# The low parts of the SSD weights: from a GpSimd subtraction to a ScalarE negation and an adding DMA

## The chip, the cores and the metric

The kernel runs on one core of a Trainium2 chip. The metric is the device time of one execution in microseconds, the median of several runs. The core has five instruction streams that run beside each other and meet through semaphores: TensorE (PE, with PEld for its weight loads), VectorE (DVE), ScalarE (ACT), GpSimd (POOL) and SyncE (SP), which only issues DMAs. DMAs can also be issued from ScalarE and GpSimd; all are carried out by the same 16 DMA engines.

## The reference: two layers of a hybrid decoder

One inference step runs 512 prompt tokens and 8 x 8 sample tokens (576 rows of width 1024) through two layers. Each layer has a token mixer between two half-step SwiGLU FFNs; layer 0 mixes with an SSD (Mamba-2) mixer, layer 1 with a pooling mixer. All is in float32. The change touches the SSD mixer:

```python
proj = h @ w_in                                   # 1024 -> 2048 (z) + 4096 (x, B, C) + 32 (dt)
xbc, conv_new = causal_dwconv(xbc, conv0, conv_w, conv_b); xbc = silu(xbc)
dt = softplus(dt_raw + dt_bias);  A = -exp(a_log)
y, ssm_new = ssd_scan(xs, dt, A, Bm, Cm, ssm0)    # 32 heads in 8 groups, chunks of 128
y = (y + d_skip * xs) * silu(z);  y = grouped_rmsnorm(y) * norm_g
return y @ w_out                                  # 2048 -> 1024
```

## The kernel before

Activations lie in SBUF with features on the 128 partitions and 576 tokens along the free dimension, in two halves of 288. A float32 product is made of three passes in a faster, rounded format (fp32r): every operand is split into a high part (the rounded value) and a low part (what the rounding left), and the matmuls are high x high, high x low and low x high. `mm` (line 334) does this: for each 128-row slice of a weight it issues six matmuls of 128x288, two halves times three products.

**Weights.** `load` (line 321) brings a slab of raw weights from HBM into one of two `raw` buffers, with a DMA from SyncE's queue. `unit` (line 328) cuts it into blocks of at most four 128x128 slices. `block` (line 311) splits one into a `wb` tile with both parts; the pool `spl` has six of them. Line 317 is ScalarE's cast to the high part, line 318 the subtraction that makes the low part, on VectorE or, where the caller says so, on GpSimd. A `wb` buffer comes free when TensorE has used it; a `raw` buffer when the low part has been made.

**The SSD stage** (`ssd`). `proj` computes 128 output features of `w_in` from the eight slices of a unit, so two blocks and 48 matmuls; 48 such units are used, 46 of them through `unit(..., G)` inside `proj` (two are prepared before, on VectorE). `outproj` adds products with `w_out` to the residual `x`: 32 units of one block, 8 of them with two slices and 24 with four. Between these, `conv_in` (lines 629 to 647) turns a projection into a convolved row block, a chain of VectorE instructions with line 645 the longest; lines 702 to 766 make the decay factors of all heads once, a chain of small 128x160 VectorE instructions (706 to 721), a spill to DRAM from ScalarE's queue (725, 727), exponentials (733, 735) and small TensorE products (746 on); and `pair` does the scan of two heads, 16 times, with masks on GpSimd (803 to 805), ten exponentials on ScalarE (808) and loads of `m`, `eb` and `nat` from SyncE's queue (795, 798, 779). `rstd` (lines 187 to 198) makes a reciprocal root by a chain of 128x5 VectorE instructions, once for each of the groups' norms.

**Order.** The program is built with `schedule_with_timeline_sim=True`: the compiler lays out the instructions of each engine in an order that it finds by simulating a timeline, and puts in the semaphores. On the chip each engine takes its stream in that fixed order, so an instruction that waits holds up all that stands behind it on its engine. Behind a weight load on SyncE's queue stand the loads of the next pair; behind a subtraction on GpSimd stand masks and small fills.

Of the kernel before, what the change touches and what calls it, by code (L numbers as in the profile page):

```python
# [8 lines left out]
F32 = mybir.dt.float32  # L9
F32R = mybir.dt.float32r  # L10
I32 = mybir.dt.int32
AF = mybir.ActivationFunctionType
ALU = mybir.AluOpType
# [4 lines left out]
P = 128  # L18
# [31 lines left out]
def trunk(ctx, tc, x_prompt, x_sample, state_ssm, state_conv, state_pool,  # L50
# [5 lines left out]
    V, S, G, PE = nc.vector, nc.scalar, nc.gpsimd, nc.tensor  # L56
# [17 lines left out]
    def acc_tile():  # L74
        return psum["acc"].tile([P, 2, 512], F32, name="acc2")

    def misc():
        return psum["misc"].tile([P, 512], F32, name="misc")
# [162 lines left out]
    def norm(pool, gname, g0):  # L241
        hhi = pool.tile([P, KD, T], F32R, name="hhi")
        hlo = pool.tile([P, KD, T], F32R, name="hlo")
        for d in range(KD):
            S.activation(out=hhi[:, d], in_=x[:, d], func=AF.Identity, scale=col(gname, g0 + d))
            V.scalar_tensor_tensor(out=hlo[:, d], in0=x[:, d], scalar=col(gname, g0 + d), in1=hhi[:, d].bitcast(F32), op0=ALU.mult, op1=ALU.subtract)
        rnorm()
        return [(hhi[:, k], hlo[:, k]) for k in range(KD)]
# [62 lines left out]
    def block(src, eng=None, pool=None):  # L311
        w = (pool or spl).tile([P, 2, 4, P], F32R, name="wb")
        k = src.shape[1]
        hi, lo = w[:, 0, 0:k], w[:, 1, 0:k]
        if src.ndim == 4:
            hi, lo = [a.rearrange("p k (c f) -> p k c f", c=src.shape[2]) for a in (hi, lo)]
        S.copy(out=hi, in_=src)  # L317
        (eng or V).tensor_tensor(out=lo, in0=src, in1=hi.bitcast(F32), op=ALU.subtract)  # L318
        return w

    def load(src, shape):
        rw = raw.tile([P, 2048], F32, name="raw")
        n = shape[0] * shape[1]
        v = rw[:, 0:n].rearrange("p (k f) -> p k f", f=shape[1])
        nc.sync.dma_start(out=v, in_=src)
        return v

    def unit(src, eng=None):
        kn = src.shape[1]
        v = load(src, src.shape[1:])  # L330
        bl = [block(v[:, k:min(k + 4, kn)], eng) for k in range(0, kn, 4)]
        return [(bl[k // 4][:, 0, k % 4], bl[k // 4][:, 1, k % 4]) for k in range(kn)]

    def mm(pt, w, acts):
        n, kn = 0, len(acts)
        for (wh, wl), (ah, al) in zip(w, acts):
            for lt, a in ((wh, ah), (wh, al), (wl, ah)):
                for h in range(2):
                    PE.matmul(out=pt[:, h, 0:HALF], lhsT=lt, rhs=a[:, h * HALF:(h + 1) * HALF],  # L339
                              start=n == 0, stop=n == 3 * kn - 1)  # L340
                n += 1

    def prep(wp, mats, n):
        st = []
        for v in mats:
            blk = [v[:, 0:4, 0:P], v[:, 4:8, 0:P], v[:, 0:4, P:2 * P], v[:, 4:8, P:2 * P]]
            s = [wp.tile([P, 4, P], F32, name="ws", bufs=6) for _ in range(4)]
            G.tensor_tensor(out=s[0], in0=blk[2], in1=blk[3], op=ALU.add)  # L348
            G.tensor_tensor(out=s[1], in0=s[0], in1=blk[0], op=ALU.subtract)  # L349
            G.tensor_tensor(out=s[2], in0=blk[2], in1=blk[0], op=ALU.subtract)  # L350
            G.tensor_tensor(out=s[3], in0=blk[1], in1=s[1], op=ALU.subtract)  # L351
            st.append([blk[0], blk[1], blk[3], s[1], s[0], s[2], s[3]])
        w = {}
        for i in range(n):
            for m, src in enumerate(st):
                w[i, m] = block(src[i])
        return st, w

    def wino(wp, pre, out, hh, done, early):
# [3 lines left out]
        def prod(i, slot):  # L363
            pt = acc_tile()
            for m in range(2):
                wb = w[i, m] if (i, m) in w else block(st[m][i])
                n = 0
                for k in range(4):
                    for j, h in ((0, 0), (0, 1), (1, 0)):
                        PE.matmul(out=pt[:, m, 0:HALF], lhsT=wb[:, j, k], rhs=hh[k, h][:, slot], start=n == 0, stop=n == 11)  # L370
                        n += 1
            return pt[:, :, 0:HALF]
# [27 lines left out]
    def kview(w):  # L400
        return w.rearrange("(k p) f -> p k f", p=P)
# [5 lines left out]
    def add_x(d, pt, scale, last):  # L407
        if scale == 1.0:
            V.tensor_tensor(out=halves(x[:, d]), in0=pt[:, :, 0:HALF], in1=halves(x[:, d]), op=ALU.add)
        else:  # L410
            V.scalar_tensor_tensor(out=halves(x[:, d]), in0=pt[:, :, 0:HALF], scalar=scale, in1=halves(x[:, d]), op0=ALU.mult, op1=ALU.add)  # L411
        if last:
            sumsq(d)
# [174 lines left out]
    def ssd(tail):  # L588
        win = kview(ssd_w_in[0])
        wout = kview(ssd_w_out[0])  # L590
        ystack = [ExitStack(), ExitStack()]
        yp = [ystack[q].enter_context(tc.tile_pool(name=f"sy{q}", bufs=2 - q, side="right", reuse_waits="tile")) for q in (1, 0)][::-1]
        yn = {}
        with ExitStack() as st:
# [5 lines left out]
            hs = norm(hp, "mix", 0)  # L600
# [22 lines left out]

            def proj(c0, w=None):
                pt = acc_tile()
                mm(pt, w or unit(win[:, :, c0:c0 + P], G), hs)
                return pt

            def conv_in(ct):
# [19 lines left out]
            for q in range(4):  # L649
# [3 lines left out]
                pt = misc()  # L653
# [4 lines left out]
            pd = acc_tile()  # L658
# [5 lines left out]
            pt = misc()  # L664
# [23 lines left out]
            for c in range(4):  # L688
                ps = slice(32 * c, 32 * c + 32)
                for t0, n, o in ((c * P, P, 0), (SEQ + 32 * c, 32, P)):  # L690
                    if t0 >= T:
                        continue
                    while n:
                        h = t0 // HALF
                        k = min(n, (h + 1) * HALF - t0)
# [48 lines left out]
            pt = misc()  # L744
# [6 lines left out]
            pt, pt2 = misc(), misc()  # L751
# [144 lines left out]
            def outproj(k0, kn, ds):  # L896
                for d in ds:
                    pd = acc_tile()
                    mm(pd, unit(wout[:, k0:k0 + kn, d * P:(d + 1) * P], G), [yn[k0 + k] for k in range(kn)])
                    add_x(d, pd, 1.0, False)  # L900

            def silu(ct, dst):
# [54 lines left out]
            def zproj(k):  # L957
                pz = proj(k * P)
                zs = wk.tile([P, T], F32, name="zs")
                V.tensor_tensor(out=halves(zs), in0=pz[:, :, 0:HALF], in1=rb2, op=ALU.mult)  # L960
                S.activation(out=zs, in_=zs, func=AF.Silu)
                return zs

            ys = None
            for g in range(8):
# [10 lines left out]
                def run(j):  # L976
                    yt = wk.tile([P, T], F32, name="yt")
                    if g % 2 == 0 and g:
                        outproj(max(2 * g - 6, 0), 4 if g > 2 else 2, range(4 * j, 4 * j + 4))
                    pair(g, j, *args, xs[j], yt)  # L980
                    nys.append(yt)
                    if j == 0 and g < 7:
                        for ct in (17 + g, 25 + g):
                            pre[ct] = conv_in(ct)
# [19 lines left out]
            for j in range(2):  # L1004
                hi, lo = yn[14 + j]
                S.activation(out=hi, in_=ys[j], func=AF.Identity, scale=col("sn", 14 + j))
                V.scalar_tensor_tensor(out=lo, in0=ys[j], scalar=col("sn", 14 + j), in1=hi.bitcast(F32), op0=ALU.mult, op1=ALU.subtract)
            accs = gsum(ys, False)
            outproj(10, 4, range(KD))
        ystack[0].close()  # L1010

# [195 lines left out]
```

## Time and profile before

| | |
|---|---|
| median of 3 runs | 2373.68 us (2372.39 to 2374.23) |
| span of the profiled execution, first to last instruction | 2369.4 us |
| SSD stage within it | about 416 to 1004 us |
| busy over the span: TensorE, VectorE, ScalarE, GpSimd | 2310.4, 1877.8, 1056.4, 1025.5 us |
| busy in the SSD stage | 575.1, 459.4, 289.4, 231.9 us of 588 |
| mean granted TensorE clock | 0.990 |

The profile is of one execution; the median is 4.3 us above its span, the time before the first and after the last instruction. "Busy" adds up the time in which an engine executes; waiting and the issuing of DMAs are not in it. The granted clock is the share of full speed that TensorE is allowed at a time; at 0.50 it runs at 1.2 instead of 2.4 GHz.

### The profile page before, as it was taken

Reading aid. Unit: us, or ns where it says so; the run is one execution under the profiler, and the core shown is the slowest. Engines: PE = TensorE matmul, PEld = TensorE weight load, DVE = VectorE, ACT = ScalarE, POOL = GpSimd, SP = SyncE. Lnnn points to the kernel's source line nnn. Section 1 sums busy time; section 2 is a strip of 40 time slices with the busy share of each in tenths; the row PEclk is TensorE's granted clock in tenths of the full one; section 3 lists DMA queues with packets and bytes.
Section 4 is the critical chain, followed back from the end, with each engine's and each line's share of the span. In section 5 each row is a group of like instructions: output and inputs, shape, how many; then the busy total and the mean of one; then the engine's idle time right before and its main releaser. Section 6 shows DMA issues by size and latency. Waiting matters only on the chain.

```text
span 2369.4 us, 43798 instructions
## 1 busy us (share of the span) xinstructions
PE 2310.4 (98%) x17572; PEld 2256.9 (95%) x17572; DVE 1877.8 (79%) x2948; ACT 1056.4 (45%) x1949; POOL 1025.5 (43%) x796
## 2 busy tenths in 40 slices
PE   8999999999999999989999999999999999999998
PEld 7999999989999999879999999999999899999997
DVE  8987777688887777799877799788776859778876
ACT  6444435355555445454443354434444344344433
POOL 4555440344434344255554435455531325555530
PEclk9999999999999999999999999999999999999998
DMA  4223222243444334322332222312322232322221
GB/s 149 90 90 107 89 81 65 71 119 114 130 119 120 106 101 128 112 72 80 99 107 72 98 90 80 107 64 90 98 81 60 70 116 86 108 69 92 89 72 59
DMA packets 272903, 222.23 MB, mean 94 GB/s; under 512 B 8321, under 2 KB 269041, under 8 KB 272700
## 3 DMA queue, kind: packets, MB, share of 16 engines
q1 hardware_dynamic: 269172, 218.04, 29.8%
q8 instruction: 139, 2.28, 0.4%
q10 hardware_dynamic: 3528, 1.39, 0.2%
q14 instruction: 64, 0.52, 0.1%
HBM read 206.46 MB, written 12.94 MB: 93 GB/s over the span
## 4 chain that ended last, share of the span: by engine, by line
PE 81%; DVE 14%; ACT 2%; issue 1%; DMA 1%; ACTq 0%; DVEq 0%; SPq 0%
PE acc L370 35%; PE acc L433 21%; PE acc L339 16%; DVE wb L318 3%; DVE wh L256 1%; PE misc L863 1%; DVE cacc L645 1%; PE acc L480 1%; PE misc L784 1%; PE misc L856 1%; DVE ws L1089 1%; PE misc L845 1%; ACT m L808 1%; PE acc L555 1%; DVE glo L256 1%
## 5 line engine op out<-in xcount | busy, mean ns | idle before, releaser
L370 PE MATMUL acc<-wh,wb 128*128 128x288 f32 x6888 | 922.4, 296 | 4.7 <-DVE fo L375 2.5
L370 PEld LDWEIGHTS acc<-wh,wb 128*128 128x128 f32 x6888 | 917.9, 189 | 6.5 <-ACT wb L317 3.0
L433 PE MATMUL acc<-ghi,wb 128*128 128x288 f32 x2752 | 482.1, 296 | 0.5 <-DVE x L411 0.5
L317 ACT CAST wb<-raw 128x512 fp32r<-128x512 f32 (+1 forms) x440 | 265.8, 608 | 350.4 <-PE acc L370 147.8
L433 PEld LDWEIGHTS acc<-ghi,wb 128*128 128x128 f32 x2752 | 406.4, 189 | 1.1 <-DVE x L411 0.9
L318 POOL TENSOR_TENSOR wb<-raw,wb 128x512 fp32r<-128x512 f32 (+1 forms) x154 | 207.5, 1350 | 346.3 <-ACT wb L317 331.2
L318 DVE TENSOR_TENSOR wb<-ws,wb 128x512 fp32r<-128x512 f32 x328 | 324.7, 1001 | 16.4 <-ACT wb L317 16.4
L339 PE MATMUL acc<-hhi,wb 128*128 128x288 f32 x1824 | 336.0, 300 | 0.8 <-DVE m L1064 0.8
L318 DVE TENSOR_TENSOR wb<-raw,wb 128x512 fp32r<-128x512 f32 (+1 forms) x286 | 270.7, 962 | 66.4 <-ACT wb L317 66.2
L317 ACT CAST wb<-ws 128x512 fp32r<-128x512 f32 x328 | 202.3, 621 | 240.4 <-PE acc L370 226.4
L433 PE MATMUL acc<-glo,wb 128*128 128x288 f32 x1376 | 294.5, 296 | 0.0
L339 PEld LDWEIGHTS acc<-hhi,wb 128*128 128x128 f32 x1824 | 272.6, 190 | 2.7 <-DVE m L1064 1.1
L411 DVE SCALAR_TENSOR_TENSOR x<-acc,x 128x576 f32<-128x576 f32 x160 | 120.6, 754 | 193.2 <-PE acc L433 193.0
L351 POOL TENSOR_TENSOR ws<-raw,ws 128x512 f32<-128x512 f32 x82 | 152.2, 1856 | 247.4 <-DVE wb L318 242.2
L318 POOL TENSOR_TENSOR wb<-rd,wb 128x512 fp32r<-128x512 f32 x128 | 175.0, 1376 | 185.4 <-ACT wb L317 185.3
L317 ACT CAST wb<-rd 128x512 fp32r<-128x512 f32 x196 | 114.2, 593 | 249.0 <-PE acc L433 222.5
L433 PEld LDWEIGHTS acc<-glo,wb 128*128 128x128 f32 x1376 | 221.6, 189 | 0.0
L339 PE MATMUL acc<-hlo,wb 128*128 128x288 f32 x912 | 202.6, 300 | 0.0
L350 POOL TENSOR_TENSOR ws<-raw 128x512 f32<-128x512 f32 x82 | 124.1, 1514 | 161.9 <-DVE wb L318 161.9
L348 POOL TENSOR_TENSOR ws<-raw 128x512 f32<-128x512 f32 x82 | 127.1, 1550 | 86.9 <-DMA raw<-in_ffn_w_gate 69.6
L339 PEld LDWEIGHTS acc<-hlo,wb 128*128 128x128 f32 x912 | 148.3, 190 | 1.2 <-issue 0.6
L349 POOL TENSOR_TENSOR ws<-ws,raw 128x512 f32<-128x512 f32 x82 | 131.6, 1605 | 8.4 <-DVE wb L318 1.5
(328 smaller groups left out, 2941.8 us busy)
## 6 DMA issues: line engine op xcount, KB each, us to landing
raw<-in_ffn_w_gate SPq DMA_DIRECT2D x41, 1024.0 KB
raw<-in_ffn_w_up SPq DMA_DIRECT2D x41, 1024.0 KB
rd<-in_ffn_w_down SPq DMA_DIRECT2D x80, 512.0 KB
raw<-in_ssd_w_in SPq DMA_DIRECT2D x48, 512.0 KB
m<-ad SPq DMA_DIRECT2D x16, 576.0 KB
nat<-in_state_ssm SPq DMA_DIRECT2D x16, 512.0 KB
out<-nat SPq DMA_DIRECT2D x16, 512.0 KB
raw<-in_ssd_w_out SPq DMA_DIRECT2D x24, 256.0 KB
```

The costliest lines, as they stand in the source:

```text
L256: V.scalar_tensor_tensor(out=o, in0=xs, scalar=g, in1=sub, op0=ALU.mult, op1=ALU.subtract)
L317: S.copy(out=hi, in_=src)
L318: (eng or V).tensor_tensor(out=lo, in0=src, in1=hi.bitcast(F32), op=ALU.subtract)
L339: PE.matmul(out=pt[:, h, 0:HALF], lhsT=lt, rhs=a[:, h * HALF:(h + 1) * HALF], start=n == 0, stop=n == 3 * kn - 1)
L348: G.tensor_tensor(out=s[0], in0=blk[2], in1=blk[3], op=ALU.add)
L349: G.tensor_tensor(out=s[1], in0=s[0], in1=blk[0], op=ALU.subtract)
L350: G.tensor_tensor(out=s[2], in0=blk[2], in1=blk[0], op=ALU.subtract)
L351: G.tensor_tensor(out=s[3], in0=blk[1], in1=s[1], op=ALU.subtract)
L370: PE.matmul(out=pt[:, m, 0:HALF], lhsT=wb[:, j, k], rhs=hh[k, h][:, slot], start=n == 0, stop=n == 11)
L411: V.scalar_tensor_tensor(out=halves(x[:, d]), in0=pt[:, :, 0:HALF], scalar=scale, in1=halves(x[:, d]), op0=ALU.mult, op1=ALU.add)
L433: PE.matmul(out=pd[:, q, 0:HALF], lhsT=lt, rhs=a[:, q * HALF:(q + 1) * HALF], start=n == 0, stop=n == 3 * kn - 1)
L480: PE.matmul(out=pd[:, m, 0:HALF], lhsT=w[:, a, 2 * k + m], rhs=b[:, h * HALF:(h + 1) * HALF], start=n == 0, stop=n == 5)
```

## The change

For the units of `proj` and `outproj`, `block` no longer subtracts. ScalarE writes the negated high part into the low part's place, and a DMA issued from GpSimd's queue adds the raw weights to it, from SBUF to SBUF (raw - high = raw + (-high)). The low part then holds all bits of the float32 difference. The other callers of `block`, with GpSimd or VectorE, stay as they were.

```diff
@@ -315,6 +315,10 @@
         if src.ndim == 4:
             hi, lo = [a.rearrange("p k (c f) -> p k c f", c=src.shape[2]) for a in (hi, lo)]
         S.copy(out=hi, in_=src)
+        if eng == "dma":
+            S.activation(out=lo, in_=hi.bitcast(F32), func=AF.Identity, scale=-1.0)
+            G.dma_start(out=lo.bitcast(F32), in_=src, accum_op=ALU.add)
+            return w
         (eng or V).tensor_tensor(out=lo, in0=src, in1=hi.bitcast(F32), op=ALU.subtract)
         return w
 
@@ -623,7 +627,7 @@
 
             def proj(c0, w=None):
                 pt = acc_tile()
-                mm(pt, w or unit(win[:, :, c0:c0 + P], G), hs)
+                mm(pt, w or unit(win[:, :, c0:c0 + P], "dma"), hs)
                 return pt
 
             def conv_in(ct):
@@ -896,7 +900,7 @@
             def outproj(k0, kn, ds):
                 for d in ds:
                     pd = acc_tile()
-                    mm(pd, unit(wout[:, k0:k0 + kn, d * P:(d + 1) * P], G), [yn[k0 + k] for k in range(kn)])
+                    mm(pd, unit(wout[:, k0:k0 + kn, d * P:(d + 1) * P], "dma"), [yn[k0 + k] for k in range(kn)])
                     add_x(d, pd, 1.0, False)
```

## Rows read from the trace of the kernel before

**Rows 1.** The profile page's first line: the span.

```profile
span 2369.4 us, 43798 instructions
```

**Rows 2.** Stretches: length, busy us by engine, granted clock, DMA share, GB/s.

```profile
470.00:490.00 20.00, 14.88 (x95) 13.16 (x94) 11.68 (x30) 8.10 (x23) 4.47 (x7) 0.74 0.29 85
...
416.00:1004.00 588.00, 575.11 (x4568) 538.05 (x4566) 459.39 (x1014) 289.39 (x617) 231.91 (x232) 0.99 0.39 112
```

**Rows 3.** TensorE's waits, 416 to 1004 us: total us, times, longest.

```profile
PE misc L746 <- DVE rhs L742: 4.7, 1, 4.7
PE misc L218 <- DVE rr L197: 4.5, 3, 2.4
PE misc L845 <- DVE xw L821: 1.3, 1, 1.3
```

**Rows 4.** Line 317, 416 to 1004 us: ns min/median/max; what its engine waited for.

```profile
L317 ACT CAST wb<-raw x129: 398/619/627, 420.2 to 1001.6; 128x512 fp32r<-128x512 f32 x121, 128x256 fp32r<-128x256 f32 x8
...
  PE acc L339: 103.7, 63
...
  DMA raw<-in_ssd_w_out: 0.6, 1
```

**Rows 5.** Groups by line, 410 to 1010 us: busy us, mean ns, idle before.

```profile
L318 POOL TENSOR_TENSOR wb<-raw,wb 128x512 fp32r<-128x512 f32 (+1 forms) x126 | 171.4, 1363 | 271.4 <-ACT wb L317 256.6 <-issue 7.8 <-DMA raw<-in_ssd_w_out 6.9
```

**Rows 6.** Timeline of VectorE, 440 to 488 us: start us, us, instruction.

```profile
449.29 1.33 DVE L706 TENSOR_SCALAR nat<-nat 128x160 f32<-128x160 f32 x1
...
454.95 1.41 DVE L712 TENSOR_TENSOR nat<-nat 128x160 f32<-128x160 f32 x1
...
457.04 0.23 DVE L713 TENSOR_SCALAR nat<-nat 128x160 f32<-128x160 f32 x1
...
457.94 0.31 DVE L712 TENSOR_TENSOR nat<-nat 128x160 f32<-128x160 f32 x1
...
461.34 1.33 DVE L713 TENSOR_SCALAR nat<-nat 128x160 f32<-128x160 f32 x1
...
466.14 1.39 DVE L713 TENSOR_SCALAR nat<-nat 128x160 f32<-128x160 f32 x1
...
467.92 1.30 DVE L715 SCALAR_TENSOR_TENSOR nat<-nat 128x160 f32<-128x160 f32 x1
```

**Rows 7.** Timeline of GpSimd, 440 to 488 us.

```profile
454.80 1.38 POOL L318 TENSOR_TENSOR wb<-raw,wb 128x512 fp32r<-128x512 f32 x1 [3.27 <-issue]
...
465.82 1.44 POOL L318 TENSOR_TENSOR wb<-raw,wb 128x512 fp32r<-128x512 f32 x1 [1.12 <-ACT wb L317]
```

**Rows 8.** Timelines of VectorE and TensorE where the chain reaches TensorE.

```profile
474.81 0.53 DVE L742 TENSOR_TENSOR rhs<-nat,mh 32x64 f32<-32x64 f32 x2
...
475.39 0.79 PE L746 MATMUL misc<-rhs,sel 64*128 64x128 f32 x2 [4.72 <-DVE rhs L742]
```

**Rows 9.** Shorter stretches, columns as in Rows 2.

```profile
480.00:482.00 2.00, 2.00 (x10) 2.00 (x11) 2.00 (x6) 0.75 (x3) 1.08 (x1) 0.50 0.03 4
...
484.00:486.00 2.00, 2.00 (x18) 1.81 (x17) 1.42 (x4) 0.00 (x0) 0.00 (x0) 1.00 0.00 0
...
926.00:956.00 30.00, 27.56 (x216) 26.30 (x215) 23.25 (x43) 16.02 (x35) 11.14 (x10) 0.94 0.40 116
```

**Rows 10.** Timelines of VectorE and GpSimd around 948 us.

```profile
947.36 0.17 DVE L193 TENSOR_TENSOR rt<-rt,rm 128x5 f32<-128x5 f32 x1
...
948.50 1.25 DVE L193 TENSOR_TENSOR rt<-rt,rm 128x5 f32<-128x5 f32 x1
...
949.99 1.10 DVE L196 TENSOR_TENSOR rt<-rt,rq 128x5 f32<-128x5 f32 x1
...
948.45 2.63 POOL L318 TENSOR_TENSOR wb<-raw,wb 128x512 fp32r<-128x512 f32 x2 [4.20 <-ACT wb L317]
```

**Rows 11.** Line 795, 416 to 1004 us: ns of one issue, min/median/max.

```profile
L795 SPq DMA_DIRECT2D m<-ad x16: 338/339/408, 474.1 to 970.6; - x16
```

**Rows 12.** The chain that ended last: start us, us, what.

```profile
646.91 3.87 DMA m<-ad
```

## Prediction

> **What bounds the kernel now.** I first read the span, then the table of stretches, then who waits for whom on TensorE, then the timeline around the longest waits. The profiled execution spans 2369.4 us [rows 1]; the median of the three timed runs, 2373.68 us, lies 4.3 us above it, which is work before the first and after the last instruction. Everything below happens inside the span, so I add its terms to the median.
>
> The change touches one stage only, the SSD mixer, from about 416 to 1004 us. There TensorE is busy 575.1 of 588 us and its clock is granted at 0.99 [rows 2]; nothing else is near that (VectorE 459, ScalarE 289, GpSimd 232 us). So the stage is bound by TensorE, and what any change can give back is its 12.9 us of idle time and the few us that its clock loses. 5.1 of the 12.9 us lie in 20 us alone, 470 to 490, where the clock is at 0.74 [rows 2].
>
> The waits of TensorE name three places, and in each it waits for VectorE: 4.7 us once for the decay factors of line 742, 4.5 us in three pieces for the reciprocal root of line 197, and 1.3 us for line 821 [rows 3]. It never waits for a weight block in that list. ScalarE's casts say the same from the other side: of 129 casts, 63 wait for TensorE to give a `wb` buffer back, and only one waits 0.6 us for a load of `ssd_w_out` [rows 4]. Weights are made early; the buffers are the limit.
>
> **What the change removes.** 46 units of `ssd_w_in` have two blocks each and 32 of `ssd_w_out` one, so 124 subtractions leave GpSimd: 116 of 128x512 and 8 of 128x256. (The row counts 126 at 1.36 us, 171 us [rows 5]; two belong to the FFN that follows.) GpSimd loses nearly all of that, but GpSimd is no bound, so by itself this is worth nothing.
>
> It is worth something on VectorE. Look at the chain that ends in the 4.7 us wait. VectorE runs without a pause from 447 to 471 us, and five of its small instructions there take over a microsecond: 1.33, 1.41, 1.33, 1.39 and 1.30 us, where the same shapes take 0.31 (two inputs) and 0.23 us (one) when they are lucky [rows 6]. GpSimd's subtractions lie beside the long ones: 454.80 to 456.18 beside the 1.41 at 454.95, 465.82 to 467.26 beside the 1.39 at 466.14 [rows 7]. So a subtraction of GpSimd can hold a VectorE instruction up for about its own length. The excess is 1.10 + 1.10 + 1.10 + 1.16 + 0.99 = 5.45 us (each less 0.23 or 0.31). The scan of line 721, the spill of line 725 and ScalarE's exponential follow in line, then line 742 at 474.81, then TensorE at 475.39 [rows 8]. TensorE waits there 4.7 us, less than the excess. **Term 1: -4.7 us**; at worst only the two-input ones recover (1.10 + 0.99 = 2.1 us), or none.
>
> The idle time costs twice, as the clock falls to half after it: at 480 to 482 us the clock is 0.50 and TensorE gets 10 matmuls done, at 484 to 486 it is 1.00 and it does 18 [rows 9]. Eight matmuls at 2/18 = 0.11 us are 0.9 us for 2 us of low clock; the low stretch in which TensorE is kept busy lasts some 3.6 us. **Term 2: -1.6 us**; 0 if some pause remains that lets the clock fall, 4.7 if all of the slow stretch counted.
>
> The same picture stands at 948 us: the root's instructions of line 193 and 196 take 1.25 and 1.10 us where their neighbours take 0.17, with two subtractions of GpSimd at 948.45 [rows 10]. That is 1.08 + 0.93 = 2.0 us in a chain whose wait on TensorE is the 2.4 us one [rows 3]; the 30 us around it ran at 0.94, so 1.8 us of clock [rows 9], of which I take half. **Term 3: -2.9 us** (0 to -3.8). The other two waits of that kind are 4.5 - 2.4 = 2.1 us together; I take half. **Term 4: -1.0 us** (0 to -2.1). Gains together: 10.2 us, at most 4.7 + 4.7 + 3.8 + 2.1 + 1.3 = 16.6 us.
>
> **What it adds on ScalarE.** 124 activations. The trace has the cast of the same shape: 0.62 us, 0.40 for half of it [rows 4]. 116 x 0.62 + 8 x 0.40 = 75 us, so ScalarE goes from 289 to 364 of 588 us. ScalarE stands still for 299 us of the stage, 104 of them in front of these very casts [rows 4], and that covers most of it: the negation follows its cast, and the next cast waits for a buffer anyway. Behind it on ScalarE wait the exponentials and copies of the pair at hand, which VectorE and then TensorE need. Without cover, one negation in each pair's way is 16 x 0.62 = 10 us. **Term 5: +2 us** (0 to +10), near the low end because TensorE's waits name no work of ScalarE [rows 3].
>
> **What it adds on GpSimd's queue and the DMA engines.** 124 issues from GpSimd, each waiting for ScalarE's negation as the subtraction waited for the cast; behind it wait the memset of the next convolution and the masks of the next pair. The trace has no DMA from GpSimd and no adding one. An issue costs between the 0.34 us of one from SyncE [rows 11] and the 1.36 us it replaces: no loss. The stage moves 112 GB/s at a DMA share of 0.39 [rows 2], 66 MB; the blocks are 116 x 262 KB + 8 x 131 KB = 31.5 MB, so copying them once adds 0.19, and if reading both operands doubles it, 0.37: 0.58 to 0.76, below full. On SyncE's queue a weight load waits until the low part has read `raw`; behind it stand the loads of `m`, `eb` and `nat` for the pair, on which masks and exponentials wait. They move as late as the low part does, below. **Term 6: +1 us** for such loads and for transfers that share the DMA engines (0 to +4).
>
> How late is the low part? Nearest row: 576 KB of `m` took 3.87 us on the chain [rows 12]. A block is less than half of that but may be read twice: I bound the transfer by about 2 us (half) and 7.8 us (double) and take 4. With negation and issue, the low part is ready 0.62 + 0.34 + 2 = 3.0 to 0.62 + 1.36 + 7.8 = 9.8 us after the cast, against 1.4. What covers it: there are six `wb` buffers and a cast runs when TensorE returns one, so five blocks lie before it: 5 x 24 x 0.11 = 13 us even if TensorE does nothing else. TensorE does not wait at any value in these bounds. The Trainium skill, DMA: Bandwidth & Descriptors, section "Anatomy of one DMA", gives 2.0 us plus bytes over 436 GB/s for a DMA issued from GpSimd; an estimate from it is 2.6 us, 3.2 with both operands. No run shown here has such a DMA; the value lies inside the bounds above and would leave the sum as it is.
>
> Sum: -10.2 + 2 + 1 = -7.2; 2373.7 - 7.2 = **2366.5 us**.
>
> **Rivals.** (a) *The gain is eaten.* The instruction order is laid out by the compiler's own timeline, so new work on ScalarE moves everything, and the new order can have pauses of its own; with term 5 at its 10 us the sum is -10.2 + 10 + 1 = +0.8: 2374.5 us. For it: VectorE's chains have no slack where they bind. Against: TensorE's 12.9 us of idle are all behind VectorE.
> (b) *VectorE stays locked out.* The issue on GpSimd takes the place of the subtraction as what holds VectorE's single-input work up. Then of term 1 only the 2.1 us of two-input work come back, the clock still falls, terms 3 and 4 (mostly two-input) bring 3: -2.1 - 3 + 3 = -2.1: 2371.6 us. The Trainium skill, SBUF — State Buffer, section "Who interferes with whom", says that VectorE in a two-port mode and GpSimd's writing of descriptors shut each other out. No row here can show it.
> (c) *The weights run out*, which ends on the other side. `raw` has two buffers, and a load waits for the low part of the unit before the last. A unit now holds its buffer for a landing of 3.9 us, four ScalarE steps of 0.62 (2.5 us) and issue plus transfer; two buffers give a unit every (6.4 + t)/2 us. TensorE takes a unit in 48 x 0.11 = 5.3 us where it does nothing else, and in 9.8 us on average (588 us over 60 units' worth of matmuls). It decides from t = 4.2 us in the dense stretches and is there everywhere from t = 13. At t = 9.2, my upper bound, a unit comes every 7.8 us, 2.5 late; if a quarter of the 46 units lie in dense stretches that is 29 us, of which the 13 us of stock cover one stretch: about +16, and with the gains halved +11: 2385 us. Against it: a cast almost never waits for a load today.
>
> **How the numbers follow.** Forecast 0.50 (2360 to 2369), (a) 0.17, (b) 0.10, (c) 0.23. A measurement tells about 0.2%, 4.7 us, from no change. The forecast lies mostly below 2369; (a) and (b) are mostly within 0.2%, (c) mostly above: faster 0.50, same 0.25, slower 0.25. The low end is the largest gain, 2373.7 - 16.6 = 2357; the high end takes in (c) with a little over its 2385: 2388. That leaves out about one in eight.
>
> **What the profile after would show.** Right: no GpSimd subtraction from `raw` in the stage; ScalarE near 364 us; VectorE's 128x160 work at 0.23 and 0.31 us; no 4.7 us wait for line 742, the clock at 1.00 around 480 us. Wrong: those instructions still over 1 us (b); ScalarE as the releaser of VectorE's waits, or a new place where TensorE stands (a); TensorE or ScalarE waiting for `raw` or for the low part (c). A transfer of over 10 us, or an order with new pauses, would break the forecast.

## Result: slower by 0.59%, and the profile after

The changed kernel took 2389.43 us (median of four runs, 2383.72 to 2391.40) against 2373.95 us: a ratio of 1.0059 (95% interval 1.0047 to 1.0070). The forecast was 2366.5 us in a range of 2357 to 2388; rival (c) had said 2385. One execution of e4 below took 5226.66 us and is left out of its ratio; as it was the profiled one, the profile is taken from e8, the same kernel once more. Lines of the code behind the edit are numbered four higher now (742 is 746, 785 is 789); line 319 is the negation, 320 the adding DMA.

The profiled execution spans 2387.9 us, 18.5 more than before. Two stretches hold all of it (11.1 and 7.9 us; the rest is 0.5 us shorter): the stage, from the start of the first product of `w_in` to that of the last of `yn` with `w_out` in line 343, and a tail from there to the first product of the next FFN, in which four more blocks of `w_out` (line 484; they don't go through the changed path) and the next norm run. Before, then after (columns as in [rows 2]):

```profile
416.80:1004.00 587.20, 574.31 (x4562) 537.25 (x4560) 459.39 (x1014) 289.39 (x617) 231.91 (x232) 0.99 0.39 112
1004.00:1024.10 20.10, 16.02 (x148) 15.13 (x146) 17.27 (x29) 11.04 (x22) 8.81 (x6) 1.00 0.25 76
```

```profile
416.70:1015.00 598.30, 581.72 (x4561) 542.96 (x4560) 399.35 (x1012) 353.32 (x740) 167.60 (x232) 0.98 0.69 163
1015.00:1043.00 28.00, 21.22 (x162) 19.34 (x160) 22.43 (x35) 13.27 (x26) 10.76 (x7) 0.84 0.18 57
470.00:490.00 20.00, 16.23 (x128) 14.96 (x126) 12.71 (x29) 11.50 (x30) 3.48 (x6) 1.00 0.48 129
```

The stage is 11.1 us longer, the tail 7.9. In the stage idle time grew from 12.9 to 16.6 us, and the same products (4562 and 4561 records) keep TensorE busy 7.4 us longer. Most of that is low clock: the trace has it at 0.50 for 13.7 us of the stage before and for 23.9 after, with TensorE busy for 11.0 and 21.4 us of these, and half of the difference is 5.2 us. Three of the low stretches, before (the first) and after, in the columns of [rows 2]:

```profile
473.30:483.50 10.20, 7.70 (x39) 6.41 (x40) 6.71 (x16) 4.44 (x10) 4.27 (x5) 0.50 0.41 118
```

```profile
866.80:873.60 6.80, 5.60 (x27) 5.35 (x29) 5.28 (x12) 5.46 (x11) 1.95 (x4) 0.50 0.87 204
1003.30:1010.10 6.80, 5.58 (x22) 4.13 (x23) 3.67 (x13) 0.00 (x0) 0.04 (x1) 0.50 0.53 155
```

Yet VectorE lost 60 us of work. At the place of term 1 (470 to 490 us) the clock is 1.00 where it was 0.74 [rows 2], though TensorE is still idle for 3.8 us there (before: 5.1), in a new place, and the clock is low behind that, from 491.3 to 494.7 us. So what VectorE was to gain came, and something larger was lost. VectorE's and TensorE's timelines there, to be held against [rows 6, 8]:

```profile
454.99 0.32 DVE L716 TENSOR_TENSOR nat<-nat 128x160 f32<-128x160 f32 x1
455.34 0.24 DVE L717 TENSOR_SCALAR nat<-nat 128x160 f32<-128x160 f32 x1
...
471.01 0.55 DVE L746 TENSOR_TENSOR rhs<-nat,mh 32x64 f32<-32x64 f32 x2
...
472.43 0.48 PE L750 MATMUL misc<-rhs,sel 64*128 64x128 f32 x2
```

The long ones are gone and TensorE doesn't wait for line 746. Who waits now: TensorE's list from 416 to 1040 us, then ScalarE's from 416 to 1004 us (total us, times, longest):

```profile
PE misc L794 <- ACT h0t L789: 6.0, 2, 3.8
PE misc L860 <- DVE ht L851: 5.0, 2, 3.2
PE acc L343 <- DVE ext L641: 3.7, 2, 3.3
```

```profile
ACT wb L317 <- PE acc L343: 44.3, 32, 3.0
ACT wb L317 <- DMA raw<-in_ssd_w_out: 38.0, 14, 6.1
ACT wb L317 <- DMA raw<-in_ssd_w_in: 35.0, 13, 6.6
...
ACT wb L317 <- DMA raw<-in_ffn_w_up: 7.8, 1, 7.8
```

[Rows 4] read the other way round: 103.7 us of waits for TensorE and 0.6 for a load. Now the casts stand 84 us for loads of weights (38.0 + 35.0 + 7.8, and 3.2 for `in_ffn_w_gate`). TensorE still waits for no weight block, so the stock of six covers the low part, as predicted. It waits, in most cases, for what stands behind a late cast in ScalarE's stream. One case, the timelines of SyncE, ScalarE and TensorE at 619 us:

```profile
612.71 5.78 SPq L329 DMA_DIRECT2D raw<-in_ssd_w_in  x2
...
618.48 1.14 ACT L317 CAST wb<-raw 128x512 fp32r<-128x512 f32 x2 [5.58 <-DMA raw<-in_ssd_w_in]
619.52 1.14 ACT L319 ACTIVATE wb<-wb 128x512 fp32r<-128x512 f32 x2
620.57 0.56 ACT L789 COPY h0t<-misc 128x512 f32<-128x512 f32 x1
...
621.19 0.65 PE L794 MATMUL misc<-h0t,ctl 128*32 128x128 f32 x8 [2.23 <-ACT h0t L789]
```

The load could not be issued before 612.71 because its buffer was still being read; the cast waits 5.58 us for it, the copy `h0t` stands behind cast and negation, and TensorE waits 2.23 us. The stops for `ht` at 587.7 and 1001.1 us are of the same kind: a cast that waits 6.15 us for `in_ssd_w_out` at 587.13, and one that waits 7.82 us for `in_ffn_w_up` at 1000.85. The stop of 3.3 us for `ext` at 864.4 us has another way, the one that term 6 named: the load of `m` stands on SyncE's queue behind two weight loads that waited for the low part (until 852.9 and 854.5 us), the exponentials wait for `m`, and VectorE for them:

```profile
855.03 0.51 SPq L799 DMA_DIRECT2D m<-ad  x1
...
861.24 1.28 ACT L812 ACT_TABLE_LOAD   x1 [1.25 <-DMA m<-ad]
...
865.08 1.23 DVE L813 TENSOR_TENSOR m<-m,cbs 128x1024 f32<-128x1024 f32 x1 [4.00 <-ACT m L812]
```

The adding DMA's own group (busy us on GpSimd, mean ns), its queue (packets, MB, share of 16 engines) and its us from issue to landing:

```profile
L320 POOL DMA_DIRECT2D wb<-raw x124 | 108.0, 883 | 292.4 <-ACT wb L319 152.6
```

```profile
q0 software_dynamic: 17856, 31.47, 7.8%
```

```profile
DMA to landing us min/median/max: 2.6/4.1/6.9
```

### The profile page after: what moved, and what is told of

It reads as the page before. It is cut to its first block, busy times and chain, and to the rows that moved or that the text cites. A ratio compares the mean times of both kernels' runs of the same rounds, so it can differ in the third digit from the quotient of the medians.

```text
span 2387.9 us, 44179 instructions
## 1 busy us (share of the span) xinstructions
PE 2321.7 (97%) x17572; PEld 2267.7 (95%) x17572; DVE 1819.3 (76%) x2948; ACT 1120.4 (47%) x2073; POOL 960.1 (40%) x796
## 3 DMA queue, kind: packets, MB, share of 16 engines
q0 software_dynamic: 17856, 31.47, 7.8%
## 4 chain that ended last, share of the span: by engine, by line
PE 80%; DVE 11%; DMA 5%; ACT 2%; issue 2%; POOL 0%; ACTq 0%; SPq 0%; DVEq 0%; POOLq 0%
PE acc L374 35%; PE acc L437 22%; PE acc L343 15%; DVE wb L322 2%; PE acc L559 2%; DMA m<-ad 2%; PE misc L867 1%; DVE wh L256 1%; DMA wb<-raw 1%; PE misc L860 1%; PE acc L484 1%; ACT m L812 1%; DVE ws L1093 1%; DMA raw<-in_ssd_w_in 0%; DVE ghi L256 0%
## 5 line engine op out<-in xcount | busy, mean ns | idle before, releaser
L322 DVE TENSOR_TENSOR wb<-ws,wb 128x512 fp32r<-128x512 f32 x328 | 322.7, 995 | 15.6 <-ACT wb L317 15.5
L320 POOL DMA_DIRECT2D wb<-raw x124 | 108.0, 883 | 292.4 <-ACT wb L319 152.6
L352 POOL TENSOR_TENSOR ws<-raw 128x512 f32<-128x512 f32 x82 | 127.9, 1559 | 85.7 <-DMA raw<-in_ffn_w_gate 68.2
```

Of the source, the lines that this page charges most:

```text
L320: G.dma_start(out=lo.bitcast(F32), in_=src, accum_op=ALU.add)
```

## Experiments

Ratios are to the kernel before, run beside each. Stage and tail are cut as above in each profile; "late" is the sum of ScalarE's waits in line 317 for loads of weights into `raw` or the added buffer, 416 to 1020 us. The kernels with three or four buffers take the added ones from a pool of their own; e5, e12, e13 and e15 make room for it by keeping a small output tile once instead of twice.

| kernel | ratio (95%) | stage us | idle in it | tail us | late us |
|---|---|---|---|---|---|
| before | 1 | 587.2 | 12.9 | 20.1 | 1.4 |
| after | 1.0059 (1.0047 to 1.0070) | 598.3 | 16.6 | 28.0 | 84.0 |
| e1 after, 3 buffers | 0.9983 (0.9974 to 0.9992) | 582.8 | 8.7 | 21.4 | 15.6 |
| e2 before, 3 buffers | 1.0001 (0.9991 to 1.0011) | 591.0 | 15.0 | 19.9 | 0 |
| e3 negation, GpSimd adds | 1.0033 (1.0020 to 1.0045) | 599.2 | 18.0 | 20.1 | 13.7 |
| e4 copy, no negation (profile: e8) | 0.9969 (0.9957 to 0.9981) | 575.0 | 4.4 | 30.1 | 18.0 |
| e5 after, 4 buffers | 1.0007 (0.9996 to 1.0018) | 582.2 | 9.0 | 29.1 | 9.0 |
| e6 VectorE subtracts | 1.0014 (1.0005 to 1.0022) | 580.2 | 8.2 | 31.7 | 8.6 |
| e7 copy, no negation, 3 buffers | 0.9942 (0.9930 to 0.9954) | 574.8 | 4.2 | 20.0 | 0 |
| e9 VectorE negates | 1.0100 (1.0085 to 1.0116) | 603.6 | 27.2 | 29.5 | 127.9 |
| e10 VectorE negates, 3 buffers | 0.9987 (0.9978 to 0.9996) | 586.1 | 13.2 | 20.0 | 6.1 |
| e11 before, side copy | 1.0075 (1.0062 to 1.0087) | 606.5 | 24.6 | 20.3 | 8.6 |
| e12 the same, 3 buffers | 1.0083 (1.0071 to 1.0096) | 605.9 | 25.2 | 19.9 | 0 |
| e13 copy, negation beside, 3 buffers | 0.9933 (0.9921 to 0.9946) | 573.2 | 2.9 | 20.1 | 0 |
| e14 before, held in order | 1.0088 (1.0076 to 1.0101) | 611.6 | 26.6 | 20.0 | 78.0 |
| e15 the same, 3 buffers | 1.0104 (1.0090 to 1.0118) | 613.3 | 29.1 | 20.3 | 4.3 |
| e16 negations shared, 3 buffers | 0.9997 (0.9987 to 1.0006) | 579.2 | 7.1 | 32.7 | 10.3 |
| e17 chained copy, 3 buffers | 0.9969 (0.9958 to 0.9981) | 578.6 | 6.1 | 21.5 | 8.5 |
| e18 chained copy | 0.9995 (0.9986 to 1.0004) | 580.1 | 6.2 | 29.4 | 38.1 |

### A third load buffer (e1, e2, e5)

```diff
-        rw = raw.tile([P, 2048], F32, name="raw")
+        rw = pool.tile([P, 1024], F32, name="rx") if pool else raw.tile([P, 2048], F32, name="raw")
...
+            rx = st.enter_context(tc.tile_pool(name="rx", bufs=1, reuse_waits="tile"))
...
+                return rx if turn[0] % 3 < 1 else None
```

> The kernel after, with a third load buffer of 4 KB for the SSD units, taken in turn with the two of raw. Theory 1 (the two load buffers are held until the adding DMA has landed, so loads start late on SyncE's queue and ScalarE's casts wait for them): most of the loss goes. SyncE's wait for the low part falls from 342 us to under 150, ScalarE's waits for raw from 73 us to under 25, and the time is 2362 to 2374 us. Theory 2 (the 75 us of negations in ScalarE's in-order stream): nothing that it names changes, 2385 to 2392 us. Theory 3 (the DMA engines are shared by more traffic, their share rose from 0.39 to 0.70): 2385 to 2392 us, and the loads take as long as now. Theory 4 (only the order laid out by the compiler is worse): any time, with ScalarE's waits for raw still near 73 us.

> The control for the run with a third load buffer: the kernel before, GpSimd subtracting, with the same third buffer. Theory 1: before, a buffer came back some 3 us after its load was cast and ScalarE waited 0.6 us for loads in all, so 2371 to 2376 us, no change. If instead it gains 5 us or more, a third buffer is worth that by itself and the run beside it says less about the DMA. Theories 2 to 4 expect no change either, up to 5 us of a new order.

The late loads fall from 84 to 16 us and the kernel is 0.76% (18 us) faster than with two buffers, faster than the kernel before too; the kernel before gains nothing from the same buffer. That speaks for theory 1, the more as the order of TensorE's and VectorE's instructions in the stage is the same but for 26 of 4559 and 6 of 1012. In the profiles the stage is 15.5 us shorter and the tail 6.6 (the rest of e1's is 4.5 us longer). The expectation for SyncE's waits was a miss: 318 us, hardly less than 342, only shared between two pools. How long that queue waits says nothing; whether the load is there when the cast wants it does.

> The kernel after with two extra load buffers of 4 KB, so four in turn (room for it comes from one small output tile kept once instead of twice, and a 64x96 tile put into another's place). Theory 1: three buffers took nearly all waits of ScalarE for loads away (73 us became less than can be seen in the list), so a fourth brings nothing more: 2367 to 2373 us. If loads still run late behind it, as the late loads of m say (GpSimd waits 65 us for them with three buffers), a fourth lets SyncE's queue run on, that wait falls under 40 us and the time is 2360 to 2367 us. Theory 2, that what is left is ScalarE: 2367 to 2373 us.

A fourth buffer leaves the stage as it is (582.2 us) and loses what the third gave in the tail; at 2374.7 us all ranges were missed. GpSimd's waits for `m` did not shrink (81 us against 65), so they are not the price of a missing buffer.

### ScalarE's share (e3, e9, e10, e16)

```diff
-            G.dma_start(out=lo.bitcast(F32), in_=src, accum_op=ALU.add)
+            G.tensor_tensor(out=lo, in0=src, in1=lo.bitcast(F32), op=ALU.add)
```

> The kernel after with the adding DMA replaced by an addition on GpSimd: ScalarE still writes all 124 negations (75 us), no DMA is added, raw is held for the negation and 1.4 us of addition. Theory 1: no long hold, so the loss goes; GpSimd again slows VectorE, so no gain over before either: 2372 to 2379 us. Theory 2: the whole loss stays, 2385 to 2392 us. Theory 3: 2372 to 2379 us, as theory 1; the run with the third buffer tells the two apart.

Half of the loss is there without any DMA, against the numbers of all three theories. It looked like ScalarE's price, so the negation went to VectorE:

```diff
-            S.activation(out=lo, in_=hi.bitcast(F32), func=AF.Identity, scale=-1.0)
+            V.tensor_scalar(out=lo, in0=hi.bitcast(F32), scalar1=-1.0, scalar2=None, op0=ALU.mult)
```

> The kernel after with the negation on VectorE (a product by -1, 0.3 to 0.7 us each, 40 to 85 us in all) in ScalarE's place; two load buffers, the DMA still adds. ScalarE is back near its 289 us, raw is held 0.6 us shorter for a block. Theory 1 (hold): ScalarE still waits over 40 us for loads of raw and most of the loss stays, 2380 to 2388 us. Theory 2 (ScalarE's 75 us): the loss goes, 2368 to 2377 us. In between, both count.

> VectorE's negation, the adding DMA and the third load buffer together: neither ScalarE's extra work nor late loads are left. If the two causes add up: 0.9983 for the third buffer, less the part of the 9.7 us between it and the copying kernel with three buffers (0.9942) that is ScalarE's, 2360 to 2368 us; it would beat both kernels. If VectorE's 40 to 85 us cost as much as ScalarE's 75: 2370 to 2376 us.

With ScalarE relieved the kernel got slower still, at 128 us of late loads (why they are later than after the change, in an order of its own, I have not settled). The third buffer brings 1.13% (27 us) here, more than anywhere, and takes the late loads to 6 us. Theory 2 has no place for that. e9's 2397.1 us is above theory 1's range too, and e10's 2369.8 us falls between its two ranges.

> The adding DMA, three load buffers, and the negations in turn on ScalarE and VectorE, 62 each. With all on ScalarE it was 0.9983, with all on VectorE 0.9987. If each engine can take some 30 us into its gaps before it costs: 2361 to 2367 us, the fastest version. If every negation costs the same wherever it is: 2368 to 2372 us.

No faster, and above both ranges (2373.4 us): its stage is the shortest of those that add (579.2 us), but its tail is 32.7 us.

### The DMA without the addition (e4, e8, e7, e13)

```diff
-            S.activation(out=lo, in_=hi.bitcast(F32), func=AF.Identity, scale=-1.0)
-            G.dma_start(out=lo.bitcast(F32), in_=src, accum_op=ALU.add)
+            G.dma_start(out=lo.bitcast(F32), in_=src)
```

> The kernel after without the negation, and with a DMA that only copies raw into the low part's place (the low part then holds the weights themselves; negation and addition are left out). ScalarE is back at its 289 us, raw is held until the copy lands. Theory 1: if the copy lands 3 to 4 us after its issue, most of the loss stays, 2378 to 2388 us, with SyncE's wait for the low part over 250 us. Theory 2: the loss goes, and the gain on VectorE shows: 2362 to 2370 us. Theory 3: fewer bytes are read, 2375 to 2388 us.

> A second look at the copying kernel with two buffers for its profile (negation and addition are left out). Theory 1: raw is held shorter than with the adding DMA, because the copy lands sooner (under 3 us from issue against 4.1) and one negation per block is gone, so that ScalarE waits under 20 us for loads of raw; if it waits over 50 us for them and the kernel is still faster than before, the hold isn't what costs.

> The copying kernel (no negation, a DMA that copies raw into the low part's place; negation and addition are left out) with the third load buffer. With two buffers it took 0.9969 of before. Theory 1 alone: the hold is what is left to lose, a third buffer gives another 5 us or more: under 2364 us. Theory 2: the hold matters only with the negations and the adding transfer on top; a third buffer gives under 3 us: 2365 to 2371 us. Against the adding kernel with a third buffer (0.9983) the difference is what the 75 us of negations and the slower adding transfer cost once loads are on time: 2 to 5 us.

e4 took 2368.2 us, in theory 2's range, though the copy landed 3.2 us after its issue (e8): without the negation that hold was not long enough to cost, and theory 1's number was a miss. e8's casts waited 11.8 us for `raw`, as expected. The stage falls to 575 us with two buffers or three, 12 us below before and more than the forecast's terms 1 to 4. The 6.5 us that the third buffer seems to give are the tail (30.1 and 20.0). e13 then wrote the negations beside, into a tile that nobody reads:

```diff
+            s = side["p"].tile([P, 4, P], F32R, name="side")[:, 0:k]
+            S.activation(out=s if src.ndim < 4 else s.rearrange("p k (c f) -> p k c f", c=src.shape[2]), in_=hi.bitcast(F32), func=AF.Identity, scale=-1.0)
+            G.dma_start(out=lo.bitcast(F32), in_=src)
```

> The copying kernel with three load buffers (0.9942) and, beside it, ScalarE's 124 negations written to a place that nobody reads (the low part holds the weights; negation and addition are left out of the result). The transfer, its landing and the load buffers are as in that kernel; only ScalarE has the 75 us more. If ScalarE's time in its stream is what costs: 2367 to 2373 us, as with the adding DMA and three buffers. If the adding transfer and the chain cast, negation, DMA is what costs: 2357 to 2362 us.

0.9933, as without them. The stage, from the table of stretches:

```profile
417.90:991.10 573.20, 570.30 (x4562) 534.10 (x4562) 399.46 (x1014) 359.63 (x743) 125.03 (x231) 1.00 0.55 170
```

ScalarE is busy 360 us (before: 289) and TensorE idle 2.9 of 573. So 70 us more on ScalarE cost nothing where nobody waits for them, and DMA engines busy to 0.55 instead of 0.39 cost nothing either. Theory 2, as put, is out; theory 3 too, as e1 beats the kernel before with the DMA engines busy to 0.72 in its stage, more than after the change (0.69).

### The hold alone, on the kernel before (e11, e12, e14, e15)

```diff
+            G.tensor_tensor(out=lo, in0=src, in1=hi.bitcast(F32), op=ALU.subtract)
+            s = side["p"].tile([P, 512], F32, name="side")
+            n = src.shape[1] * P
+            G.tensor_copy(out=s[:, 0:8], in_=lo[:, 0, 0:8].bitcast(F32))      # e14, e15 only
+            G.dma_start(out=s[:, 0:n].rearrange("p (k f) -> p k f", f=P), in_=src)
```

> The kernel before with the hold of raw alone made longer: after GpSimd's subtraction a DMA from GpSimd copies the block of raw to a place that nobody reads, so raw is held for 1.4 us of subtraction, 0.55 of issue and some 3.2 us of landing, like in the kernel after (0.6 + 0.9 + 4.1), and the DMA engines carry the same 31.5 MB. ScalarE's work and the low part are as before. Theory 1: ScalarE waits over 40 us for loads of raw and the time is 2384 to 2396 us, as much as a third buffer gave back in the kernel after (18 us). Theory 2: no ScalarE work is added, 2371 to 2378 us. Theory 3 (traffic): slower too, which the run beside it decides.

> The same with the third load buffer. Theory 1: the loss of the run beside it goes but for GpSimd's longer work (0.55 us of issue a block): 2373 to 2380 us. Theory 3, that the DMA traffic is what costs: no change against the run beside it.

e11 met theory 1's number for another reason: its casts were late by 9 us only. The compiler had put the side copy ahead of the subtraction, and GpSimd stood 178 us for loads of `raw` itself. A third buffer changed nothing there (e12).

> The kernel before with raw held longer, once more: GpSimd subtracts, copies eight columns of the low part to the side place (which forces the order), and then issues the DMA that copies the block of raw over it. Theory 1: ScalarE waits over 40 us for loads of raw and the time is 2384 to 2400 us. If it waits under 15 us for them, two buffers bear this hold, and what is lost is GpSimd's longer work: 2376 to 2386 us.

> The same with the third load buffer. Theory 1: at least half of the loss of the run beside it goes, 2374 to 2384 us, and ScalarE's waits for loads with it. No change against the run beside it if the loss is GpSimd's work or the DMA traffic.

Now the casts are late as after the change (e14, ScalarE's waits):

```profile
ACT wb L317 <- DMA raw<-in_ssd_w_in: 46.0, 14, 7.2
...
ACT wb L317 <- DMA raw<-in_ssd_w_out: 24.0, 13, 5.1
```

But the third buffer takes these away and the time stays (1.0104). In these kernels GpSimd does 108 us more (39 of small copies, 69 of issues), and TensorE's waits name VectorE again (10.2 us for line 197 in e14). The pair failed to isolate the hold: these kernels lose their time elsewhere, and in them late casts are not what is last.

### Adding or copying, in one order (e17, e18)

```diff
-            G.dma_start(out=lo.bitcast(F32), in_=src, accum_op=ALU.add)
+            G.dma_start(out=lo.bitcast(F32), in_=src)
```

> The kernel after with the third load buffer and a DMA that copies raw over the negation and does not add (the low part then holds the weights; the addition is left out). The chain cast, negation, DMA and the 75 us on ScalarE are as with the adding DMA. If the addition is what costs the 10.7 us between the two kernels with three buffers: 2357 to 2363 us. If the chain does: 2366 to 2373 us.

> The same with two load buffers: only the addition is taken from the kernel after (the low part holds the weights). If the longer hold by the addition (0.33 us of issue and 1 us of landing a block) made the loads late: ScalarE waits under 30 us for raw in place of 73, 2362 to 2373 us. If the chain alone makes them late: over 50 us of waits and 2380 to 2390 us.

This pair decides. e17 took 2367.2 us, in the range for the chain; e18 took 2373.2 us with 30.4 us of waits for `raw`, both just over the bounds for the hold and far from those for the chain. The instruction streams of all five engines are the same, instruction for instruction, in e18 and in the kernel after, and in e17 and e1; only the transfer differs. With two buffers the addition costs 1.0059 / 0.9995, 0.64% or 15 us (12 to 19 by the two intervals); with three 0.14%, 3.3 us, which is hardly clear of noise (0 to 7). Adding instead of copying changes three things at once: the hold, GpSimd's time for the issues (41 us more) and the share of the DMA engines (0.69 instead of 0.55). With three buffers the latter two are there as well, so it is the hold, with two buffers, that costs most of the 15 us. e18's stage, tail, late loads and landing:

```profile
417.80:997.90 580.10, 573.92 (x4561) 537.07 (x4560) 399.51 (x1012) 355.37 (x740) 127.58 (x232) 0.99 0.55 168
997.90:1027.30 29.40, 22.67 (x160) 20.81 (x159) 22.33 (x35) 13.22 (x26) 10.70 (x7) 0.79 0.18 54
```

```profile
ACT wb L317 <- DMA raw<-in_ssd_w_in: 15.8, 7, 4.2
...
ACT wb L317 <- DMA raw<-in_ssd_w_out: 14.6, 8, 4.7
```

```profile
DMA to landing us min/median/max: 1.9/2.8/6.7
```

At the place shown above (619 us in the kernel after) e18's loads go out at 609.22, 3.5 us sooner (the transfer that held the buffer took 3.3 us there and 5.2 after the change, from issue to landing); the same casts wait for TensorE, not for a load, and `h0t` goes to TensorE in time:

```profile
613.40 1.14 ACT L317 CAST wb<-raw 128x512 fp32r<-128x512 f32 x2 [2.15 <-PE misc L218]
614.45 1.15 ACT L319 ACTIVATE wb<-wb 128x512 fp32r<-128x512 f32 x2
615.50 0.56 ACT L789 COPY h0t<-misc 128x512 f32<-128x512 f32 x1
```

### VectorE subtracts (e6)

```diff
-                mm(pt, w or unit(win[:, :, c0:c0 + P], G), hs)
+                mm(pt, w or unit(win[:, :, c0:c0 + P], V), hs)
```

(and the same in `outproj`)

> The kernel before with VectorE in GpSimd's place for the subtractions of the SSD units: no DMA, no negation, no subtraction of GpSimd. VectorE pays 116 x 0.69 + 8 x 0.42 = 83 us and gets back the 82 us or so by which GpSimd's subtractions stretched its other work, so it stays near 459 us busy. Raw is held as short as can be (0.62 + 0.69 us a block). Theory 1 (holds count) and theory 2 (ScalarE counts): no worse than before, 2366 to 2376 us. If instead VectorE's own chains bind (every wait of TensorE names VectorE), each subtraction that comes between costs: 2376 to 2390 us.

The stage is 7 us shorter than before, though VectorE is busy 477 us between 416 and 1004 us (before: 459); the tail is 11.6 us longer. Nothing is won in all (0.14% slower).

## Why the prediction was wrong

**Terms 1 to 4 (-10.2 us) held as a sum.** Without GpSimd's subtractions the stage falls by 12 to 14 us where nothing else is in the way (e7, e13), and in e13 TensorE waits neither for line 742's work nor for the root of line 197. I compared each VectorE instruction of the stage with the shortest of its line and shape: before, 77 were over 0.3 us longer, 68.3 us together, 64.2 of it beside line 318; after, 13 with 11.0 us. None of these lay beside a DMA issue alone, though GpSimd was busy 108 us with those: that is against rival (b). The Trainium skill, SBUF — State Buffer, section "Who interferes with whom", says that a VectorE instruction with two inputs in SBUF contends with a GpSimd instruction that reads SBUF; the rows before agree (1.41 us beside a subtraction, 0.31 elsewhere [rows 6, 7]). The same section of the Trainium skill says that VectorE in a two-port mode and GpSimd's descriptor writing block each other; none of the 124 issues shows this on VectorE's side.

Term 1 came in part only: behind the vanished wait TensorE stops 3.8 us at 486 us for `h0t` (e13: 1.0). Term 2 was too small: it counted 3.6 us of work at the low clock, where TensorE is busy 7.7 us at 0.50 (the row from 473.30 above), so 3.8 us are lost there and not 1.6.

**Term 5 (+2 us for ScalarE) was right as busy time, too small as a link.** Beside the path the negations cost nothing (e13). In the chain cast, negation, DMA they put the issue off: e17 against e13 is 0.9969 to 0.9933, 8.5 us, and e3 against the kernel before, where only the negation is put into the chain, is 0.33%, 7.8 us. Both compare two different orders, so part of it may be order.

**Term 6 (+1 us, 0 to +4) is the step that failed.** In one and the same order adding instead of copying alone cost 15 us. "On SyncE's queue a weight load waits until the low part has read `raw`" was the right place, and rival (c) the right mechanism; it was given 0.23 and "a cast almost never waits for a load today" as evidence against, a row that speaks of a hold of 1.4 us. By rival (c)'s own working, 4 us of transfer and an issue of 0.34 us or more are already above its 4.2, yet the sum went on as if below.

That 4.2 was itself misread. The 18 records of [rows 9] between 484 and 486 us are mostly products of 128 columns, and some began before; a weight product of 128x288 starts every 0.133 us where TensorE is dense (36 in 5.06 us in the row from 1005.50 below). A unit of `w_in` then takes 48 x 0.133 = 6.4 us, not 5.3, one of `w_out` with four slices 24 x 0.133 = 3.2 us, and the stock of five blocks is 16 us, not 13. The other side was misjudged the other way: the hold is not four ScalarE steps and a transfer, as negation and issue also wait in the fixed orders of ScalarE and GpSimd. From a unit's first cast to the landing of its last DMA it took, in the median, 9.4 us for `w_in` and 5.9 for `w_out` with four slices (e18: 8.2 and 4.4; before, to the end of the last subtraction: 6.0 and 2.0). With the landing of the load, 4.4 and 2.9 us (e18: 4.0 and 2.9), two buffers give a unit every 6.9 and 4.4 us (e18: 6.1 and 3.7). For `w_in` TensorE's pace lies between the two kernels; for `w_out` both are late, the adding one by more than twice as much. These are medians, and part of the hold is a cast that waits for TensorE, so they show the direction and not the microseconds.

What rival (c) mis-sized besides is the price. A unit that is a little late was to cost little, with the stock before it; but the stock holds weights, and TensorE stopped for `h0t`, `ht` and `ext`, which come behind the waiting cast or the late load of `m`. Each stop then cost a second time at low clock: between e18 and the kernel after, idle time in the stage is 10.4 us of the 18.2, busy time 7.8 (e18 has 6.8 us at low clock, after the change it is 23.9). The stops at 587.7, 618.7, 864.4 and 1001.1 us (from one product's start to the next, less the usual pitch) are 11.1 us together, and each has a stretch at 0.50 behind it; in e18 three of them are left, at 589.0, 857.0 and 989.0, with 2.7 us and none.

The estimate of 2.6 us from the Trainium skill, DMA: Bandwidth & Descriptors, section "Anatomy of one DMA", was near the copy's 2.8 us (e18); the adding DMA took 4.1.

**Rival (a)'s other half, an order with pauses of its own, came true in the tail.** Its 7.9 us are not the transfer: e18, with the copy in the same order, has 29.4. TensorE's timeline, before and after:

```profile
1005.50 5.06 PE L480 MATMUL acc<-yn,wb 128*128 128x288 f32 x36
1010.40 0.38 PE L236 MATMUL misc<-ident,rr 128*128 128x128 f32 x2
```

```profile
1021.67 1.58 PE L484 MATMUL acc<-yn,wb 128*128 128x288 f32 x10
...
1025.53 0.43 PE L236 MATMUL misc<-ident,rr 128*128 128x128 f32 x2 [2.07 <-DVE rr L197]
...
1038.24 3.25 PE L484 MATMUL acc<-yn,wb 128*128 128x288 f32 x12 [2.74 <-DVE e L460]
```

Before, 36 products stand between the sums of squares and line 236 and cover VectorE's chain; after, 26 of them are placed among the sums and ten are left, so TensorE waits 2.07 us; with that, the wait before it (0.73 us) and the one after it (2.74, before 2.5) the clock is at 0.84 in the tail (before: 1.00). The e5, e9, e16 and e18 profiles have this order, e6 and e8 much the same one, and the tails of all six are 29 to 33 us.

The profile's account: -7.1 us for the stage with a copying chain (e18 against before), +18.2 for adding with two buffers, +9.3 for the tail's order, -1.4 in the tail between e18 and the kernel after: 19.0, against the 18.5 of the spans. In timed runs, against the kernel before: -15.9 us with the copy and the negation beside (e13), -7.4 with the negation in the chain (e17), -1.2 with two buffers and the slow tail (e18), +14.0 with the addition. That e17 meets the forecast's -7.2 us is luck: a larger gain against a larger price on ScalarE. What stays open: why the compiler's order of the tail differs from build to build, how much of the 8.5 us between e17 and e13 is order, and where e3 loses its 8 us; its TensorE waits (3.9 us for `ch`, 2.9 for `rhs`, 2.6 for `ext`) name no one cause.

The fastest versions that leave nothing out are e1 and e10, 0.9983 and 0.9987: the change pays, by 3 to 4 us, once a third load buffer, 4 KB on each partition, goes with it.

## What to carry to other kernels

When a step is moved to a slower carrier, work out how long it holds its *source* buffer, not only when its result is due: load plus hold, divided by the number of buffers, against the consumer's pace. Count in the hold what each step waits in the order of its engine, and take the pace from the start of one product of that shape to the next, not from a count in a short window. If the two are near each other, everything behind the loader and the caster in their fixed orders becomes late, not only the weights. Test a claim on a planned program with a kernel whose order is the same to the last instruction; seven of the kernels here lost 8 to 13 us through an order of the tail alone. Long waits of a queue that only loads ahead are no cost in themselves (SyncE still waited 318 us for the low part in e1).

## What the runs showed of the hardware

The 124 DMAs from GpSimd that add within SBUF (256 KB each, eight of them 128) made about twice the packets of plain copies (17856 in the kernel after against 9664 in e18, for the same 31.47 MB), kept the 16 engines more than twice as long (7.8% against 3.6% of the span) and GpSimd 0.88 us an issue against 0.54, and landed after 4.1 us against 2.8. Beside the issues alone no VectorE instruction of the stage was over 0.3 us longer than the shortest of its kind; beside GpSimd's subtractions, before, such instructions lost 64.2 us.
